# Gate and up weights of each expert loaded whole, one after the other, and multiplied in two 256-column passes

## The chip, the core and the metric

The kernel runs on one core of one Trainium2 chip. The metric is the device time of one execution in microseconds, the median of several runs. TensorE (PE) does the matmuls, VectorE (DVE) and ScalarE (ACT) the elementwise work, GpSimd (POOL) a few copies, and SyncE (SP) issues nearly all transfers from HBM. PE's weight loads have a row of their own in the profile (PEld).

## What is computed

One decoder block: a mixer (two kinds of attention), then a mixture of experts over 256 tokens with 64 experts, of which each token takes 8, and a shared expert; then a final norm. The change touches the experts:

```python
def swiglu(x, w_gate, w_up, w_down):
    return (jax.nn.silu(x @ w_gate) * (x @ w_up)) @ w_down

def moe_ffn(xt, ...):
    ...  # scores, top-k experts eidx and weights wts of each token, rows sorted by expert
    def body(acc, bidx):
        rows = ...; wr = ...; e = blk_expert[bidx]
        ye = swiglu(xt[rows], w_gate_e[e], w_up_e[e], w_down_e[e]) * wr[:, None]
        return acc.at[rows].add(ye.astype(acc.dtype)), None
    routed, _ = lax.scan(body, jnp.zeros_like(xt), jnp.arange(n_blk))
    return routed + swiglu(xt, w_gate_sh, w_up_sh, w_down_sh)
```

Of one expert, gate and up are 1024 x 256 float32 each (1 MB each) and down is 256 x 1024 (1 MB). All 64 experts are read: 201 MB of the 267 MB that the kernel moves.

## The kernel before

The first 270 us or so compute the mixer. Then come the experts in 26 tiles, numbered 0 to 25 here. A tile has 128 rows of PSUM, shared out among two experts (64 + 64 rows, or 96 + 32) or four experts (32 rows each; tiles 3, 7, 11, 15, 20 and 25). Experts are ranked by their load, so that from tile 3 on the expert's number is read from `order` at run time. Ten tiles are worked in four column groups of 32 (the six with four experts, and the four with 96 + 32, whose 96 is cut in three); the other sixteen in two groups of 64.

Two things run side by side.

- **SP** loads weights in program order (`load_tile`, L1086) into a ring of 1 MB buffers (`w8`, L127; 20 of them from tile 3 on, each a [128, 2048] float32 tile: `w`, `whi`, `wlo`, `hh`, `g2r`, `xs`, `gr`, `vv` and `sr` in the profile's names). Expert row p*8+j goes to partition p, so that a partition's gate weights are 8 KB in a row in HBM. `load_gu` (L160) is called for the halves h = 0 and 1: it takes one buffer, and fills its first half with rows j = 4h to 4h+3 of gate and its second half with the same rows of up, each a transfer of 512 KB with 4 KB in a row per partition. So gate and up of an expert are four transfers into two buffers. `load_dn` (L166) loads down as one transfer of 1 MB with 8 KB in a row. A transfer waits until its buffer was last read, and until the transfer eight before it on SP has landed, since SP's transfers take eight completion semaphores in turn.
- **PE** runs the tiles. A tile's steps are, in PE's order: `tile_up` (L1122, eight j, and for each the column groups side by side, a float32 matmul of 512 columns that does gate and up at once), `slot_map` (L1132), `scatter` of the tile before (L1188), `gather` of the next tile's tokens (L1058), the two transposes of `hidden_T` (L1002) and `down` (L1169). `swiglu` (L990) runs on ACT and DVE when the last matmul of `tile_up` is done. A float32 matmul shows in the trace as two matmul records and two weight loads.

The first four j of `tile_up` read the buffers of h = 0, the last four those of h = 1. The last tile loads in smaller pieces (L1095 to L1106), and its down weights in three column cuts (`load_dn_cuts`, `last_down`), so that the end of the kernel waits for little. `late_expert` (L945) is a loop for experts whose tokens overflow their rows; its trip count is zero for these inputs.

Of the kernel before, what the change touches and what calls it, by code (L numbers as in the profile page):

```python
# [25 lines left out]
FF = 256  # L26
# [82 lines left out]
def block_kernel(ctx: ExitStack, tc: tile.TileContext, x, c, norm1_g, norm2_g, w_ada, b_ada, w_in,  # L109
                 w_branch_sb, w_branch_mb, w_out, w_router, router_bias, w_gate_e, w_up_e, w_down_e,  # L110
                 w_gate_sh, w_up_sh, w_down_sh, rel_bias, final_g, const_a, const_m, const_b, out):
    nc = tc.nc
    P = 128
    mm = nc.tensor.matmul
# [9 lines left out]
    def k8(tag, shape, dtype=F32):  # L124
        return wk.tile(shape, dtype, name=tag, tag=tag, bufs=SIZES.get(tag, 1))

    def w8():  # L127
        ring.append(ring.pop(0))
        return k8(ring[-1], [P, 2048])
# [4 lines left out]
    def small(parts=P, width=512, dtype=F32):  # L134
        return wk.tile([parts, width], dtype, name="mg", tag="mg", bufs=4)
# [21 lines left out]

    ss2 = consts.tile([P, 10], F32, name="ss2")

    def load_gu(wg, wu, h):  # L160
        w = w8().rearrange("p (g j f) -> p g j f", g=2, j=4)
        nc.sync.dma_start(w[:, 0], wg.rearrange("(p j) f -> p j f", j=8)[:, 4 * h:4 * h + 4])
        nc.sync.dma_start(w[:, 1], wu.rearrange("(p j) f -> p j f", j=8)[:, 4 * h:4 * h + 4])
        return [w[:, :, j, :] for j in range(4)]

    def load_dn(wd):  # L166
        w = w8().rearrange("p (j n) -> p j n", j=2)
        nc.sync.dma_start(w, wd.rearrange("(p j) n -> p j n", j=2))
        return w

    h2, h2v, hp3, r1, h2T, scores_ = [], [], [], [], [], []
# [23 lines left out]
    with ExitStack() as pa:  # L195
# [534 lines left out]
        for i, ticks in enumerate(ROW_AT):  # L730
            n = 4 + i
# [75 lines left out]
    def rot():  # L807
        return ps.tile([P, 512], F32, name="rot", tag="rot", bufs=3)

    def gub():  # L810
        return ps.tile([P, 512], F32, name="gu", tag="gu", bufs=1)

    def sm(name, shape, dtype=F32, bufs=1):
        return wk.tile(shape, dtype, name=name, tag=name, bufs=bufs)
# [129 lines left out]
    def late_expert(k):  # L944

        no = sm("no", [1, 2], I32)
        nc.sync.dma_start(no[:, 0:1], ranks_d[:, bass.ds(k, 1)])
        rank_ = nc.values_load(no[0:1, 0:1], engines=[EN.SP], min_val=0, max_val=NE - 1)
        nc.sync.dma_start(no[:, 1:2], order_d[:, bass.ds(rank_, 1)])
        col = sm("col", [P, 4])  # L950
        nc.sync.dma_start(col, late_d[:, bass.ds(rank_, 1)].rearrange("p o q -> p (o q)"))
        ev = nc.values_load(no[0:1, 1:2], engines=[EN.SP], min_val=0, max_val=NE - 1)
        wg, wu, wd = (w[0, bass.ds(ev, 1)].rearrange("o a b -> (o a) b") for w in (w_gate_e, w_up_e, w_down_e))
        gu = load_gu(wg, wu, 0) + load_gu(wg, wu, 1)
        wd = load_dn(wd)
        for first in (0, 128):
            one = small().rearrange("p (t s) -> p t s", t=4)[:, 0:2]
            for t in range(NT):
                nc.vector.tensor_scalar(one[:, t], iota1, float(first), col[:, t:t + 1], op0=OP.add, op1=OP.is_equal)
            S = wk.tile([P, NT, 128], BF, name="S", tag="zs", bufs=4)  # L960
            nc.vector.tensor_copy(S, one)
            xg = gather(len(TILES), S)
            pq = rot()
            for t in range(NT):
                nc.tensor.transpose(pq[:, t * 128:(t + 1) * 128], one[:, t], ident)
            for t in range(NT):
                mm(pq[:, 256:257], one[:, t], col[:, 2 + t:3 + t], start=t == 0, stop=t == 1, skip_group_check=True)
            ST = wk.tile([P, 256], F32R, name="ST", tag="e", bufs=3)
            wsl = sm("wsl", [P, 1], bufs=2)
            nc.vector.tensor_copy(ST, pq[:, 0:256])  # L970
            nc.vector.tensor_copy(wsl, pq[:, 256:257])
            p = gub()
            for j in range(8):
                mm(p, xg[:, j], gu[j], start=j == 0, stop=j == 7)
            at = hidden_T(swiglu(p))
            scatter(ST, down(at, [wd], [(0, 128, 0)], wsl))

    shp, shw = {}, {}

    def load_shared():  # L980
        shw["gu"] = load_gu(w_gate_sh[0], w_up_sh[0], 0) + load_gu(w_gate_sh[0], w_up_sh[0], 1)

    def load_shared_down():
        shw["d"] = load_dn(w_down_sh[0])
# [11 lines left out]
    def shared_up(t, j0, j1):  # L996
        if j0 == 0:
            shp[t] = rot() if t else gub()
        for j in range(j0, j1):
            mm(shp[t], h2T[0][:, j, t * 128:(t + 1) * 128], shw["gu"][j], start=j == 0, stop=j == 7)  # L1000

    def hidden_T(sg, at=None):  # L1002
        pt = rot()
# [82 lines left out]
    def load_tile(i):  # L1086
        n = len(TILES[i])
        es = []
        for _, r in TILES[i]:
            if r < NFIX:  # L1090
                es.append([w[0, r] for w in (w_gate_e, w_up_e, w_down_e)])
            else:
                ev = nc.values_load(order[0:1, r:r + 1], engines=[EN.SP], min_val=0, max_val=NE - 1)
                es.append([w[0, bass.ds(ev, 1)].rearrange("o a b -> (o a) b") for w in (w_gate_e, w_up_e, w_down_e)])
        if i == len(TILES) - 1:  # L1095

            gu = [load_gu(e[0], e[1], 0) for e in es]
            ws = [w8().rearrange("p (g j f) -> p g j f", g=2, j=4) for e in es]
            for j in (0, 2):
                for w, e in zip(ws, es):  # L1100
                    for g in range(2):
                        nc.sync.dma_start(w[:, g, j:j + 2],
                                          e[g].rearrange("(p j) f -> p j f", j=8)[:, 4 + j:6 + j])
            for g, w in zip(gu, ws):
                g += [w[:, :, j, :] for j in range(4)]
            return gu, load_dn_cuts([e[2] for e in es])  # L1106
        gu = [[] for s in range(n)]
        for h in range(2):
            for s in range(n):
                gu[s] += load_gu(es[s][0], es[s][1], h)  # L1110
        return gu, [load_dn(e[2]) for e in es]

    def groups(i):

        out, c0 = [], 0
        for s, (cap, _) in enumerate(TILES[i]):
            for n in (32, 32, 32) if cap == 96 else (cap,):
                out.append((c0, n, s))
                c0 += n
        return out  # L1120

    def tile_up(i, xg, gu, between=()):  # L1122
        p = gub()
        for j in range(8):
            if j == 4:
                for f in between:
                    f()
            for c0, n, s in groups(i):
                mm(p[c0:c0 + n, :], xg[:, j, c0:c0 + n], gu[s][j], start=j == 0, stop=j == 7, skip_group_check=True)  # L1129
        return swiglu(p)  # L1130

    def slot_map(i):  # L1132
# [55 lines left out]
    def scatter(ST, ys):  # L1188
        for c, y in zip(HALVES, ys):
            scatter_cut(ST, y, c)  # L1190
# [12 lines left out]


    load_shared()
    shared_up(0, 0, 5)
    tokens_T(1, rot)
    shared_up(0, 5, 6)
# [15 lines left out]
    xg = gather(0, S)  # L1224
# [45 lines left out]
    for i in range(len(TILES)):  # L1270
# [4 lines left out]
        gu, wd = load_tile(i)  # L1275
# [6 lines left out]
        else:  # L1282
# [5 lines left out]
            if i:  # L1288
                xg = gather(i + 1, S)
# [5 lines left out]
        else:  # L1295
            prev = ST, down(at, wd, groups(i), wsl)
            if i == 0:
                xg = gather(i + 1, S)
# [33 lines left out]
```

## Time and profile before

| what | value |
|---|---|
| time, median of 3 runs | 750.12 us (749.75 to 750.17) |
| the profiled execution | 748.62 us, of which its span is 746.5 us |
| PE busy | 696.3 us of the span (93%), 4727 matmul records |
| DMA moved | 266.73 MB, 357 GB/s over the span |
| experts' stage, about 275 us to the end | DMA engines busy throughout, about 410 GB/s |

All times below are microseconds from the span's start. A "busy" PE row means that a matmul is in its pipeline. A DMA share above 1.00 comes of packets that overlap a little on one engine. The landing of a transfer isn't a row of its own, but in the stretch where SP waits for landings the distance of its issues is the distance of the landings.

### The profile page before, as it was taken

The page shows a single profiled execution, that of the slowest core. Times are in us where ns is not written, and L with a number is a line of the kernel's source. Part 1 is how long each engine was busy: PE and PEld are TensorE (multiplying, and loading weights), DVE is VectorE, ACT ScalarE, POOL GpSimd, SP SyncE. Part 2 cuts the span into 40 slices and gives each one's busy share as a digit, 9 for nine tenths or more (in the row PEclk, how much of TensorE's full clock was granted, in tenths as well). Part 3 has the DMA queues.
Part 4 walks back from the last instruction along what each step waited for, and adds up shares of the span by engine and source line. Part 5 has one row for each costly group of instructions (what it writes and reads, how often), then busy time and mean ns, then how long its engine had stood idle before and what let it go on. Part 6 is the DMA issues. An engine that isn't in the chain of part 4 may idle for free.

```text
span 746.5 us, 12489 instructions
## 1 busy us (share of the span) xinstructions
PE 696.3 (93%) x4727; PEld 389.5 (52%) x4727; DVE 312.3 (42%) x663; ACT 202.3 (27%) x332; POOL 25.1 (3%) x37
## 2 busy tenths in 40 slices
PE   3799999999999979999999999999999998899994
PEld 0486677667787645544444444444444453445532
DVE  1365766766667342333333233332242332223323
ACT  2354665465743231111111111011111110111122
POOL 1010001000001050000000000000000000000000
PEclk9999999999999998999999999999999999999998
DMA  9999988776658659999999999999999999999994
GB/s 352 412 380 389 375 285 301 253 270 217 240 210 297 250 216 383 375 382 413 409 414 413 413 410 396 411 411 412 415 412 412 413 412 414 406 410 412 406 333 157
DMA packets 76862, 266.73 MB, mean 357 GB/s; under 512 B 7013, under 2 KB 9221, under 8 KB 67968
## 3 DMA queue, kind: packets, MB, share of 16 engines
q1 hardware_dynamic: 75344, 262.24, 90.9%
q0 software_dynamic: 1312, 3.65, 1.5%
q8 instruction: 39, 0.64, 0.3%
q14 instruction: 23, 0.19, 0.1%
q10 hardware_dynamic: 144, 0.00, 0.0%
HBM read 264.68 MB, written 1.19 MB: 356 GB/s over the span
## 4 chain that ended last, share of the span: by engine, by line
PE 53%; DMA 41%; DVE 2%; ACT 1%; SPq 1%; issue 1%; POOL 1%; DVEq 0%; ACTq 0%
PE gu L1129 9%; PE big L264 7%; PE big L267 7%; PE big L265 7%; DMA w<-in_w_up_e_dram 6%; DMA w<-in_w_gate_e_dram 5%; DMA whi<-in_w_gate_e_dram 5%; PE rot L1069 5%; PE rot L1153 4%; DMA w<-in_w_ada_dram 3%; DMA whi<-in_w_down_e_dram 3%; PE acc L1185 3%; DMA g2r<-in_w_gate_e_dram 3%; DMA vv<-in_w_down_e_dram 2%; PE att L412 2%; DMA g2r<-in_w_up_e_dram 2%
## 5 line engine op out<-in xcount | busy, mean ns | idle before, releaser
L1129 PE MATMUL gu<-w,hl 128*32 128x512 f32 (+1 forms) x552 | 108.1, 594 | 1.5 <-DMA w<-in_w_up_e_dram 1.4
L264 PE MATMUL big<-whi,hh 128*128 128x512 f32 x184 | 75.0, 408 | 1.7 <-ACT whi L384 1.7
L1153 PE MATMUL rot<-w,at 128*32 128x512 f32 (+1 forms) x272 | 69.6, 629 | 5.7 <-DVE at L1008 5.7
L265 PE MATMUL big<-whi,hl 128*128 128x512 f32 x184 | 72.6, 395 | 0.0
L993 DVE TENSOR_TENSOR sg<-sg,gu 128x256 f32<-128x256 f32 x27 | 11.4, 421 | 140.5 <-ACT sg L992 140.5
L1165 ACT ACTIVATE mg<-y 128x512 fp32r<-128x512 f32 x51 | 32.1, 630 | 130.4 <-DVE y L1159 130.4
L1069 PE MATMUL rot<-S,qksb 128*128 128x128 bf16 x600 | 66.4, 219 | 0.0
L1159 DVE SCALAR_TENSOR_TENSOR y<-rot,wsl,gate 128x512 f32<-128x512 f32 (+1 forms) x53 | 39.1, 738 | 65.0 <-PE rot L1153 63.8
L1069 PE MATMUL rot<-S,qkmb 128*128 128x128 bf16 x600 | 66.1, 219 | 0.0
L1129 PEld LDWEIGHTS gu<-w,hl 128*32 128x32 f32 (+1 forms) x552 | 32.3, 121 | 57.5 <-issue 53.2
L246 DVE TENSOR_TENSOR wlo<-w,whi 128x2048 fp32r<-128x2048 f32 x23 | 52.7, 2291 | 20.1 <-ACT whi L245 19.1
L267 PE MATMUL big<-wlo,hh 128*128 128x512 f32 x184 | 54.0, 394 | 0.2 <-DVE wlo L246 0.2
L1185 PE MATMUL acc<-mg,ST 128*128 128x512 f32 x204 | 54.1, 406 | 0.0
L1166 DVE TENSOR_TENSOR mg<-y,mg 128x512 fp32r<-128x512 f32 x51 | 35.3, 693 | 38.5 <-ACT mg L1165 38.5
L1073 ACT ACTIVATE hl<-rot 128x512 f32<-128x512 f32 x26 | 15.5, 597 | 127.9 <-PE rot L1069 127.9
L992 ACT ACTIVATE sg<-gu 128x256 f32<-128x256 f32 x27 | 10.3, 383 | 136.1 <-PE gu L1129 136.1
L1185 PEld LDWEIGHTS acc<-mg,ST 128*128 128x128 f32 x204 | 36.3, 188 | 17.4 <-ACT sg L992 9.1
L245 ACT ACTIVATE whi<-w 128x2048 fp32r<-128x2048 f32 x23 | 43.9, 1910 | 5.0 <-PE big L265 5.0
L1069 PEld LDWEIGHTS <-qksb 128*128 128x128 bf16 x600 | 40.9, 98 | 7.2 <-issue 6.1
L264 PEld LDWEIGHTS big<-whi,hh 128*128 128x128 f32 x184 | 34.9, 190 | 17.1 <-issue 3.8
L1069 PEld LDWEIGHTS <-qkmb 128*128 128x128 bf16 x600 | 42.0, 98 | 0.0
L1129 PE MATMUL gu<-gr,hl 128*64 128x512 f32 (+1 forms) x104 | 39.6, 593 | 0.5 <-DMA gr<-in_w_up_e_dram 0.5
(354 smaller groups left out, 1103.8 us busy)
## 6 DMA issues: line engine op xcount, KB each, us to landing
w<-in_w_gate_e_dram SPq DMA_DIRECT2D x58, 512.0 KB, 12.0
w<-in_w_up_e_dram SPq DMA_DIRECT2D x58, 512.0 KB, 12.3
w<-in_w_down_e_dram SPq DMA_DIRECT2D x28, 1024.0 KB, 12.0
w<-in_w_ada_dram SPq DMA_DIRECT2D x24, 1024.0 KB, 12.5
w<-in_w_in_dram SPq DMA_DIRECT2D x16, 1024.0 KB, 13.0
whi<-in_w_gate_e_dram SPq DMA_DIRECT2D x12, 512.0 KB, 11.9
whi<-in_w_up_e_dram SPq DMA_DIRECT2D x12, 512.0 KB, 12.1
wlo<-in_w_down_e_dram SPq DMA_DIRECT2D x6, 1024.0 KB, 11.3
```

Source lines behind the costliest of these rows:

```text
L245: nc.scalar.activation(hi, w, AF.Copy)
L246: nc.vector.tensor_tensor(lo, w, hi.bitcast(F32), op=OP.subtract)
L264: mm(p, aa[i][0], ww[i][0], start=start and i == 0, stop=False)
L265: mm(p, aa[i][1], ww[i][0], start=False, stop=False)
L267: mm(p, aa[i][0], ww[i][1], start=False, stop=stop and i == n - 1)
L1069: mm(p[:, b * 128:(b + 1) * 128], parts[k][:, half * 4 + b, :], S[:, k * NT // n], start=k == 0, stop=k == n - 1)
L1129: mm(p[c0:c0 + n, :], xg[:, j, c0:c0 + n], gu[s][j], start=j == 0, stop=j == 7, skip_group_check=True)
L1153: mm(py[c0:c0 + w, 0:n], at[:, jj, c0:c0 + w], wd[s][:, jj, o:o + n], start=jj == 0, stop=jj == 1, skip_group_check=True)
L1159: nc.vector.scalar_tensor_tensor(y, py[:, 0:n], wsl, gate2[:, o:o + n], op0=OP.mult, op1=OP.mult)
L1165: nc.scalar.activation(yh, y, AF.Copy)
L1166: nc.vector.tensor_tensor(yl, y, yh.bitcast(F32), op=OP.subtract)
L1185: mm(sums(t, c), m if len(y) > 1 else m.bitcast(F32), part, start=False, stop=stop and k == len(y) - 1, skip_group_check=True)
```

## The change

Each expert's gate becomes one transfer of 1 MB with 8 KB in a row, into a buffer of its own, and so does up. A tile loads the gates of all its experts first, then the ups, then the downs. `tile_up` then does the eight j of gate into columns 0 to 255 of the tile's PSUM bank, and after them the eight j of up into columns 256 to 511: sixteen steps of 256 columns instead of eight of 512. The new function `up_cut` holds one such step; `gu` is now a list of pairs (gate, up) of buffers. What `between` runs (the last tile's `scatter` and `final_gain`, and `by_expert` in tile 0) stands between the passes, after the same number of PE columns as before. The shared expert and the late loop use the same functions. In the last tile gate is loaded whole, and up as j 0 to 3, then 4 and 5, then 6 and 7.

```diff
-    def load_gu(wg, wu, h):
-        w = w8().rearrange("p (g j f) -> p g j f", g=2, j=4)
-        nc.sync.dma_start(w[:, 0], wg.rearrange("(p j) f -> p j f", j=8)[:, 4 * h:4 * h + 4])
-        nc.sync.dma_start(w[:, 1], wu.rearrange("(p j) f -> p j f", j=8)[:, 4 * h:4 * h + 4])
-        return [w[:, :, j, :] for j in range(4)]
+    def load_gu(wg, wu):
+
+        ws = [w8().rearrange("p (j f) -> p j f", j=8) for _ in range(2)]
+        for w, d in zip(ws, (wg, wu)):
+            nc.sync.dma_start(w, d.rearrange("(p j) f -> p j f", j=8))
+        return ws
+
+    def up_cut(p, xg, gu, gs, k):
+
+        g, j = divmod(k, 8)
+        for c0, n, s in gs:
+            mm(p[c0:c0 + n, FF * g:FF * g + FF], xg[:, j, c0:c0 + n], gu[s][g][:, j, :], start=j == 0, stop=j == 7,
+               skip_group_check=True)
...
     def shared_up(t, j0, j1):
         if j0 == 0:
             shp[t] = rot() if t else gub()
-        for j in range(j0, j1):
-            mm(shp[t], h2T[0][:, j, t * 128:(t + 1) * 128], shw["gu"][j], start=j == 0, stop=j == 7)
+        for k in range(2 * j0, 2 * j1):
+            up_cut(shp[t], h2T[0][:, :, t * 128:(t + 1) * 128], [shw["gu"]], [(0, 128, 0)], k)
...
         if i == len(TILES) - 1:
 
-            gu = [load_gu(e[0], e[1], 0) for e in es]
-            ws = [w8().rearrange("p (g j f) -> p g j f", g=2, j=4) for e in es]
-            for j in (0, 2):
-                for w, e in zip(ws, es):
-                    for g in range(2):
-                        nc.sync.dma_start(w[:, g, j:j + 2],
-                                          e[g].rearrange("(p j) f -> p j f", j=8)[:, 4 + j:6 + j])
-            for g, w in zip(gu, ws):
-                g += [w[:, :, j, :] for j in range(4)]
+            gu = [[w8().rearrange("p (j f) -> p j f", j=8) for g in range(2)] for e in es]
+            for g, o, m in ((0, 0, 8), (1, 0, 4), (1, 4, 2), (1, 6, 2)):
+                for w, e in zip(gu, es):
+                    nc.sync.dma_start(w[g][:, o:o + m], e[g].rearrange("(p j) f -> p j f", j=8)[:, o:o + m])
             return gu, load_dn_cuts([e[2] for e in es])
-        gu = [[] for s in range(n)]
-        for h in range(2):
-            for s in range(n):
-                gu[s] += load_gu(es[s][0], es[s][1], h)
+        gu = [[w8().rearrange("p (j f) -> p j f", j=8) for g in range(2)] for e in es]
+        for g in range(2):
+            for w, e in zip(gu, es):
+                nc.sync.dma_start(w[g], e[g].rearrange("(p j) f -> p j f", j=8))
         return gu, [load_dn(e[2]) for e in es]
...
         p = gub()
-        for j in range(8):
-            if j == 4:
+        for k in range(16):
+            if k == 8:
                 for f in between:
                     f()
-            for c0, n, s in groups(i):
-                mm(p[c0:c0 + n, :], xg[:, j, c0:c0 + n], gu[s][j], start=j == 0, stop=j == 7, skip_group_check=True)
+            up_cut(p, xg, gu, groups(i), k)
         return swiglu(p)
```

On SP, a tile of two experts took ten transfers. This is tile 0, whose experts have fixed numbers; in later tiles rows that only set a register stand between. Before:

```order
L162 DMA w_2121<-in_w_gate_e_dram 128x1024
L163 DMA w_2121<-in_w_up_e_dram 128x1024
L162 DMA w_2124<-in_w_gate_e_dram 128x1024
L163 DMA w_2124<-in_w_up_e_dram 128x1024
L162 DMA w_2127<-in_w_gate_e_dram 128x1024
L163 DMA w_2127<-in_w_up_e_dram 128x1024
L162 DMA w_2130<-in_w_gate_e_dram 128x1024
L163 DMA w_2130<-in_w_up_e_dram 128x1024
L168 DMA w_2133<-in_w_down_e_dram 128x2048
L168 DMA w_2135<-in_w_down_e_dram 128x2048
```

The same tile on SP in the changed kernel:

```order
L1113 DMA w_2135<-in_w_gate_e_dram 128x2048
L1113 DMA w_2137<-in_w_gate_e_dram 128x2048
L1113 DMA w_2136<-in_w_up_e_dram 128x2048
L1113 DMA w_2138<-in_w_up_e_dram 128x2048
L176 DMA w_2143<-in_w_down_e_dram 128x2048
L176 DMA w_2145<-in_w_down_e_dram 128x2048
```

Six transfers of 1 MB stand where there were eight of 512 KB and two of 1 MB; the bytes and the count of buffers are the same.

On PE, this is the middle of `tile_up` of tile 20 (four experts), where it passes from the first 4 MB of its weights to the second; `hl` holds the gathered tokens. Before:

```order
L1129 MATMUL gu<-w_5649,hl 32x512
L1129 MATMUL gu<-w_5652,hl 32x512
L1129 MATMUL gu<-w_5655,hl 32x512
L1129 MATMUL gu<-whi,hl 32x512 x2
L1129 MATMUL gu<-wlo,hl 32x512 x2
L1129 MATMUL gu<-hh,hl 32x512
```

The same place in the changed kernel:

```order
L171 MATMUL gu<-w_6015,hl 32x256
L171 MATMUL gu<-w_6017,hl 32x256
L171 MATMUL gu<-whi,hl 32x256
L171 MATMUL gu<-wlo,hl 32x256
L171 MATMUL gu<-w_6016,hl 32x256
L171 MATMUL gu<-whi,hl 32x256
L171 MATMUL gu<-wlo,hl 32x256
L171 MATMUL gu<-hh,hl 32x256
```

The first rows of each are the last step that reads the first 4 MB, the later ones the first step that reads the second 4 MB. The seam stands at the same place in PE's work, and each step has half the columns.

## Rows read from the trace of the kernel before

**Rows 1.** Page, span in 40 slices: busy tenths of the DMA engines, GB/s.

```profile
DMA  9999988776658659999999999999999999999994
GB/s 352 412 380 389 375 285 301 253 270 217 240 210 297 250 216 383 375 382 413 409 414 413 413 410 396 411 411 412 415 412 412 413 412 414 406 410 412 406 333 157
```

**Rows 2.** Windows: stretch, length; busy us and records of each engine; PEclk, DMA share, GB/s.

```profile
340.00:360.00 20.00, 19.48 (x202) 8.67 (x198) 7.11 (x17) 2.88 (x5) 0.00 (x0) 1.00 1.02 412
360.00:540.00 180.00, 172.95 (x1432) 81.84 (x1426) 58.20 (x126) 22.42 (x40) 0.00 (x0) 1.00 1.02 410
...
620.00:660.00 40.00, 34.55 (x271) 16.25 (x268) 10.70 (x23) 3.88 (x7) 0.00 (x0) 1.00 1.02 410
...
710.00:720.00 10.00, 9.48 (x74) 3.58 (x71) 4.05 (x8) 1.86 (x3) 0.20 (x1) 1.00 0.91 310
720.00:730.00 10.00, 8.47 (x58) 3.14 (x59) 0.85 (x2) 2.86 (x4) 0.00 (x0) 1.00 1.04 357
```

**Rows 3.** Chain that ended last, in order of time: start, us, what (from tile 19).

```profile
605.71 6.87 PE gu L1129 x32
...
615.27 2.70 PE rot L1069 x48
...
626.04 14.99 DMA vv<-in_w_down_e_dram
...
641.05 10.05 DMA w<-in_w_up_e_dram
...
723.89 8.11 DMA hh<-in_w_down_e_dram
```

**Rows 4.** Windows, columns as Rows 2: `tile_up` of tile 20, of tile 21.

```profile
622.36:634.67 12.31, 9.25 (x66) 2.47 (x64) 1.96 (x3) 0.63 (x1) 0.00 (x0) 1.00 1.02 416
...
644.62:654.85 10.23, 8.35 (x35) 2.79 (x36) 1.95 (x3) 0.63 (x1) 0.00 (x0) 1.00 1.01 410
```

**Rows 5.** Waits of SP, 300 to 740 us: waiter, awaited: us in total, times, longest.

```profile
SPq L162 <- DMA w<-in_w_down_e_dram: 26.4, 13, 2.1
...
SPq L162 <- PE rot L1153: 15.5, 2, 8.4
```

**Rows 6.** Timeline of SP: start, us, transfer issued (two stretches).

```profile
364.14 0.33 SPq L162 DMA_DIRECT2D g2r<-in_w_gate_e_dram  x1
...
375.64 0.33 SPq L168 DMA_DIRECT2D sr<-in_w_down_e_dram  x1
...
538.07 0.33 SPq L163 DMA_DIRECT2D w<-in_w_up_e_dram  x1
...
548.03 0.33 SPq L163 DMA_DIRECT2D w<-in_w_up_e_dram  x1
```

**Rows 7.** Page: transfers issued, KB each, median us from issue to landing.

```profile
w<-in_w_gate_e_dram SPq DMA_DIRECT2D x58, 512.0 KB, 12.0
...
w<-in_w_down_e_dram SPq DMA_DIRECT2D x28, 1024.0 KB, 12.0
```

**Rows 8.** Engines; instruction queue of the span, and of 360 to 700 us (DMA).

```profile
PE 696.3 (93%) x4727; PEld 389.5 (52%) x4727; DVE 312.3 (42%) x663; ACT 202.3 (27%) x332; POOL 25.1 (3%) x37
...
q8 instruction: 39, 0.64, 0.3%
...
q8 instruction: 21, 0.34, 0.4%
```

**Rows 9.** Timeline of PE: float32 matmuls of 256 columns, two and four groups.

```profile
705.06 0.59 PE L1139 MATMUL rot<-qkmb,ca 64*64 64x256 f32 x4
...
732.29 0.38 PE L1153 MATMUL rot<-hh,at 128*32 128x256 f32 x1
...
732.50 0.59 PE L1153 MATMUL rot<-hh,at 128*32 128x256 f32 x2
```

**Rows 10.** Timeline of PE after a wait for a landing: first and twelfth record.

```profile
538.16 0.14 PEld L1129 LDWEIGHTS gu<-vv,hl 128*32 128x32 f32 x2 [1.62 <-issue]
...
538.24 0.11 PEld L1129 LDWEIGHTS gu<-gr,hl 128*32 128x32 f32 x1
```

More of the change, by code (lines that the diff above doesn't have):

```diff
@@ L953, in late_expert @@
         wg, wu, wd = (w[0, bass.ds(ev, 1)].rearrange("o a b -> (o a) b") for w in (w_gate_e, w_up_e, w_down_e))
-        gu = load_gu(wg, wu, 0) + load_gu(wg, wu, 1)
+        gu = load_gu(wg, wu)
         wd = load_dn(wd)
@@ L972, in late_expert @@
             p = gub()
-            for j in range(8):
-                mm(p, xg[:, j], gu[j], start=j == 0, stop=j == 7)
+            for k in range(16):
+                up_cut(p, xg, [gu], [(0, 128, 0)], k)
             at = hidden_T(swiglu(p))
@@ L980, in load_shared @@
     def load_shared():
-        shw["gu"] = load_gu(w_gate_sh[0], w_up_sh[0], 0) + load_gu(w_gate_sh[0], w_up_sh[0], 1)
+        shw["gu"] = load_gu(w_gate_sh[0], w_up_sh[0])
     def load_shared_down():
@@ L1123, in tile_up @@
         p = gub()
-        for j in range(8):
-            if j == 4:
+        for k in range(16):
+            if k == 8:
                 for f in between:
                     f()
-            for c0, n, s in groups(i):
-                mm(p[c0:c0 + n, :], xg[:, j, c0:c0 + n], gu[s][j], start=j == 0, stop=j == 7, skip_group_check=True)
+            up_cut(p, xg, gu, groups(i), k)
         return swiglu(p)
```

## The prediction

> **What bounds the kernel now.** I read the page's slices first. From about 280 us to 710 us the DMA engines are busy in every slice at about 410 GB/s [rows 1], and by the windows at a share of 1.02 [rows 2]. The reader is to see that the experts' weights are one unbroken stream, which can end earlier only if its bytes pass faster. PE is busy 173 of 180 us in the same stretch [rows 2], so it is nearly bound too, and the question is which of the two ends last. The chain of waits answers it: it runs on PE through tile 19 (`tile_up` 6.87 us there), and from 626 us on transfers, the last of them landing at 723.89 + 8.11 = 732.0 us [rows 3]. The windows of single tiles show what PE loses: `tile_up` took 12.31 us in tile 20 and 10.23 us in tile 21 [rows 4] against 6.87 us where nothing is awaited [rows 3], so 5.4 + 3.4 = 8.8 us of waiting for weights. I estimate 1.5 us more in the last tile. So about 10.3 us is what a much faster stream could give; beyond it PE binds.
>
> What paces the stream? SP waits mostly for landings (26.4 us in its largest group) and for a buffer only early, 15.5 us in two waits [rows 5], while transfers take 12 us from issue to landing [rows 7]: there is always work queued. So the pace of landings is the price of a byte. From 364.14 to 375.64 us SP issues nine transfers after the first, each let go by the landing of a 512 KB piece: 11.50 / 9 = 1.278 us for a piece with 4 KB in a row. From 538.07 to 548.03 us it issues four, each let go by a down of 1 MB with 8 KB in a row: 9.96 / 4 = 2.490 us [rows 6].
>
> **The change part by part.**
>
> *Long rows.* Two pieces of 512 KB take 2 x 1.278 = 2.556 us, one of 1 MB 2.490 us: 0.066 us per MB less, 0.132 us per expert, since gate and up are 2 MB. Gate and up become transfers of the very shape that down has now, into the same buffers, so I take the price of down's rows for them in full. The lower end is nothing (the 2.5% is a property of the down tensor), the upper is the 10.3 us above. Counted up to where PE last waits in the middle of the kernel, tile 21's second half: tiles 3 to 20 hold 46 experts, tile 21 two, so 48 x 0.132 = 6.3 us. (Tiles 0 to 2 are loaded before the stream is unbroken, behind the mixer's own work, and count as nothing.)
>
> [...] The rows show 2.6%, and down's transfers are the same on the same queue, so I go by them.
>
> *Instruction fetch.* This is what the change adds to the stream. Each 256-column step is a matmul of its own, and a float32 matmul is two matmul and two load records: `tile_up` had 16 x 16 + 10 x 32 = 576 matmuls, the shared expert 16, so 592 x 4 = 2368 records more. The run had 4727 + 4727 records of PE and the page counts 39 fetches of instructions [rows 8], so a fetch brings some 240 records, and 2368 are about 10 fetches more, 8 of them before tile 21's weights. What does one cost the stream? In 340 us there were 21, which took 0.4% of 16 engines: 0.004 x 340 x 16 / 21 = 1.04 us of one engine each [rows 8]. If they spread evenly the stream loses 1.04 / 16 = 0.065 us; if they always hit the engine that is last it loses all of it. Between: an expert without disturbance is 2 x 2.556 + 2.490 = 7.60 us for 3.146 MB, 414 GB/s, and the window shows 410 [rows 2], 1% or 3.3 us in 340, so 0.16 us per fetch. I take that: 8 x 0.16 = 1.3 us. Ends: 0.5 and 8.3 us.
>
> *The second pass on PE.* A step of 512 columns takes 6.87 / 16 = 0.429 us per record (sixteen records deep, the groups side by side) [rows 3]. Steps of 256 columns stand in the trace too: with two groups, two steps of 64 x 64 end in 0.59 us, of which the last one's own length is 0.38, so 0.21 us apart; with four groups 732.29 to 732.50 us, also 0.21 [rows 9]. Read as 0.215, two of them are 0.43, the price of the one they replace. I take +0.1 us per tile (ends 0 and 0.3). Until tile 20 PE's waits swallow it; after the last wait five tiles are left, 0.4 us with what falls in the last tile. The weight loads double, but one lasts 0.11 to 0.14 us [rows 10] and lies under a step of 0.21.
>
> *Waits and order.* The first pass needs the gates of all the tile's experts, 1 MB each, where the first four j needed a buffer of 1 MB of each: the same bytes at the same place in the queue, and buffers come free at the same two points. So no new wait, at nothing; the cover is that the seam in `tile_up` stays in its middle. With eight transfers of 1 MB in flight in place of 4.8 MB on average, SP looks further ahead, and waits for buffers more; that costs only if the stream runs dry, and 8 MB in flight say it doesn't. Four fewer issues per tile of two experts save SP 0.33 us each [rows 6], off the path. `swiglu` still waits for the last matmul of the tile, so ACT starts no sooner.
>
> *The last tile.* Now sixteen pieces of 256 KB follow each other there, and with eight in flight the stream thins out: 310 GB/s and 357 GB/s in the last two windows against 410 [rows 2]. Eight of the sixteen become four of 512 KB. The 4 MB of the second half then need about 10.5 us in place of 11.7, an estimate from these rates, so the last weights gain 1 us more than the middle ones. Down's cuts stay. PE comes to them earlier by its own gain alone, so of this I count 0.3 us.
>
> **Sum.** At tile 21's second half the stream is ahead by 6.3 - 1.3 = 5.0 us, which is within the 5.4 + 3.4 us that PE waits there, so PE moves by it. From there PE adds 0.4 us and the last tile gives back 0.3: 5.0 - 0.4 + 0.3, about 4.9 us. The profiled execution, 748.62 us, would become 743.7. The median shown is 750.12, 1.5 us above that execution, so I forecast 750.12 - 4.9 = **745.2 us**.
>
> **The rivals.**
>
> *Fetches eat the gain (slower).* One mechanism: each added fetch holds up one DMA engine, and the landing waits for the last of 16. It decides at 6.3 / 8 = 0.79 us per fetch. For it: 1.04 us is what one takes of its engine. Against it: 21 fetches cost 3.3 us, not 21. At 1.04 us the stream is 8.3 - 6.3 = 2.0 us later, with PE's 0.4 about 752.5 us; at half of that, 0.5 us, it still gains, 747.9.
>
> *PE becomes the bound by issue (slower).* In a tile of four groups `tile_up` goes from 128 to 256 records in 6.9 us, 27 ns each. The longest stretches of the trace show no more than 400 records in 20 us, 50 ns each [rows 2]. If that were the limit of PE's sequencer, such a tile would go from about 330 records in 16.7 us to 460 in 23, 6.3 us more in each of ten tiles, less the 10.3 us of slack: near 800 us. It decides at about 37 ns per record. Against it: after a wait, twelve records start within 0.1 us (538.16 to 538.24 us) [rows 10], and the gather does 48 matmuls with 48 loads in 2.70 us, 28 ns a record [rows 3].
>
> [...]
>
> *The rows don't pay.* If gate and up keep 2.556 us per MB, 1.3 us of fetches and 0.4 us of PE are left: about 751 us, no change. Nothing in the trace speaks for it but that only down has been seen with 8 KB rows.
>
> *More than forecast.* Fetches at 0.065 us, and the disturbances that 4 KB packets meet fall away with them: up to the 10.3 us, 740 us.
>
> **How the numbers follow.** Forecast (742 to 748) 0.62; more than forecast (740 to 742) 0.08; fetches 0.14, of which 0.04 still end more than 0.2% faster, 0.05 within and 0.05 slower; rows don't pay 0.08, of which 0.06 within 0.2% and 0.02 slower; issue limit 0.04, slower; price per matmul 0.04, within. 0.2%, 1.5 us, is about what a measurement of this kernel can tell from no change. So faster 0.62 + 0.08 + 0.04 = 0.74, within 0.05 + 0.06 + 0.04 = 0.15, slower 0.05 + 0.02 + 0.04 = 0.11. The range runs from 740.0, where PE binds, to 750.0, which takes in most of the cases without change.
>
> **What the profile after would show.** Issues of SP in its waiting stretch 2.49 us apart throughout, and 411 to 416 GB/s in the middle windows: the long rows pay. `tile_up` still 6.9 us where nothing is awaited, in tiles of two and of four groups: PE's term is right; 8 us or more in four-group tiles alone would be the issue limit. `tile_up` of tiles 20 and 21 at about 7.5 and 10 us: PE took over the stream's gain. About 49 fetches on the page, and a rate below 408 GB/s with landings at 2.49: the fetches. The forecast is wrong if gate and up land at 2.55 us per MB, or if the stream runs dry between tiles.

## The result and the profile after

| | before | changed |
|---|---|---|
| median of the runs made side by side, us | 749.93 (748.60 to 750.17) | 740.70 (740.62 to 741.19) |
| ratio, with its 95% interval | | 0.9867 (0.9840 to 0.9894) |
| profiled execution, us (span) | 748.62 (746.5) | 740.65 (738.8) |

The kernel became 9.2 us faster. The forecast was 745.2 us, a gain of 4.9: the sign was right and the time lies in the range, but the gain is almost twice the one that was summed up.

The first fence is from the page after the change: the slices of the DMA engines and GB/s, and the queue of instruction fetches (they answer to [rows 1, 8]).

```profile
DMA  9999988777566769899999999999999999999993
GB/s 351 414 386 385 364 262 300 252 266 266 214 212 237 291 229 425 341 381 422 419 420 420 419 419 421 420 422 418 421 419 422 421 419 422 418 421 419 420 346 125
...
q8 instruction: 48, 0.79, 0.4%
```

The second is windows of the changed kernel, with the columns of [rows 2]: the stream's middle, `tile_up` of tile 20 and of tile 21, and two windows near the end of the stream.

```profile
340.00:700.00 360.00, 345.46 (x3677) 211.03 (x3670) 119.58 (x269) 46.05 (x83) 1.60 (x3) 1.00 1.01 420
619.67:626.78 7.11, 7.11 (x134) 4.12 (x136) 1.96 (x3) 0.63 (x1) 0.00 (x0) 1.00 1.01 418
636.96:647.01 10.05, 7.99 (x67) 4.67 (x68) 1.94 (x3) 0.63 (x1) 0.00 (x0) 1.00 1.01 419
700.00:710.00 10.00, 9.48 (x123) 5.50 (x124) 4.10 (x7) 1.86 (x3) 0.20 (x1) 1.00 0.93 348
710.00:720.00 10.00, 9.04 (x105) 4.73 (x97) 1.06 (x4) 2.15 (x4) 0.00 (x0) 1.00 1.01 357
```

The stream moves 420 GB/s where it moved 410 [rows 2], with its engines as full as before (a share of 1.01, where it was 1.02): the same occupation carries more bytes. `tile_up` of tile 20 waits for nothing any more (12.31 us became 7.11 [rows 4]), and tile 21's wait of 3.0 us is what is left (10.05, against 7.08 in the tiles after it).

SP's timeline shows the pace by itself, as in [rows 6]. From the first of these three rows to the last are nine issues, each let go by a landing of 1 MB, gates, ups and downs alike: 22.36 / 9 = 2.484 us.

```profile
600.25 0.33 SPq L1113 DMA_DIRECT2D wlo<-in_w_up_e_dram  x1
...
612.66 0.33 SPq L176 DMA_DIRECT2D vv<-in_w_down_e_dram  x1
...
622.61 0.33 SPq L1113 DMA_DIRECT2D w<-in_w_up_e_dram  x1
```

The chain that ended last has changed sides. Before, it lay on transfers from tile 20 to the last down cut [rows 3]. Now its last transfer is an up of tile 21, landing at 643.29 us (622.61 + 20.69 before rounding), and from there PE runs to the end without waiting for a weight.

```profile
602.74 19.75 DMA hh<-in_w_up_e_dram
...
622.61 20.69 DMA w<-in_w_up_e_dram
...
643.34 3.67 PE gu L171 x30
...
656.89 6.91 PE gu L171 x64
...
707.83 3.59 PE gu L171 x64
```

### The profile page after: what moved, and what is told of

It reads as the page before. It is cut to its first block, busy times and chain, and to the rows that moved or that the text cites. A ratio compares the mean times of both kernels' runs of the same rounds, so it can differ in the third digit from the quotient of the medians.

```text
span 738.8 us, 14329 instructions
## 1 busy us (share of the span) xinstructions
PE 690.3 (93%) x5911; PEld 449.7 (61%) x5911; DVE 312.1 (42%) x663; ACT 202.1 (27%) x332; POOL 25.4 (3%) x37
## 4 chain that ended last, share of the span: by engine, by line
PE 76%; DMA 17%; DVE 3%; ACT 1%; issue 1%; POOL 1%; SPq 0%; DVEq 0%; ACTq 0%
PE gu L171 19%; PE rot L1155 10%; PE rot L1077 8%; PE big L272 7%; PE big L275 7%; PE big L273 7%; PE acc L1187 6%; DMA w<-in_w_up_e_dram 5%; DMA hh<-in_w_up_e_dram 5%; DMA w<-in_w_ada_dram 4%; DMA w<-in_w_down_e_dram 3%; PE att L420 2%; PE rot L1141 2%; PE acc L1032 1%; PE rot L171 1%; DVE at L1016 1%
## 5 line engine op out<-in xcount | busy, mean ns | idle before, releaser
L171 PE MATMUL gu<-w,hl 128*32 128x256 f32 (+1 forms) x1136 | 118.2, 380 | 1.6 <-DMA w<-in_w_up_e_dram 1.2
L171 PEld LDWEIGHTS gu<-w,hl 128*32 128x32 f32 (+1 forms) x1136 | 69.6, 121 | 40.4 <-issue 6.9
L1155 PE MATMUL rot<-w,at 128*32 128x512 f32 (+1 forms) x272 | 67.2, 610 | 5.7 <-DVE at L1016 5.7
L171 PE MATMUL gu<-whi,hl 128*64 128x256 f32 (+1 forms) x208 | 46.4, 380 | 0.0
L171 PE MATMUL gu<-wlo,hl 128*32 128x256 f32 (+1 forms) x256 | 42.7, 379 | 0.0
```

Of the source, the lines that this page charges most:

```text
L171: mm(p[c0:c0 + n, FF * g:FF * g + FF], xg[:, j, c0:c0 + n], gu[s][g][:, j, :], start=j == 0, stop=j == 7, skip_group_check=True)
L1155: mm(py[c0:c0 + w, 0:n], at[:, jj, c0:c0 + w], wd[s][:, jj, o:o + n], start=jj == 0, stop=jj == 1, skip_group_check=True)
```

## The experiments

Two numbers come back in what follows. The **stretch** is the time from the landing of tile 5's last down to that of tile 24's last down, worked out from each transfer's issue and its time to landing: 46 experts' gate and up and 47 downs (the shared expert's among them), the unbroken part of the stream. Its **lateness** sums up the landings in it that came late: those more than 0.12 us over the median spacing of their kind (a piece of gate or up, or a down), each by what it was over that median. The fetches are those of instructions in the whole span, as the page counts them. Stretch and lateness are of one profiled execution, in us, and the time is the median of the runs.

| kernel | gate and up as | fetches | stretch | lateness | time |
|---|---|---|---|---|---|
| before | 512 KB, 4 KB rows | 39 | 358.16 | 6.6 | 749.93 |
| before_again | the same | 39 | 356.09 | 4.3 | 749.39 (one run) |
| short_rows | the same | 48 | 356.82 | 5.0 | 748.72 |
| big_short | 1 MB, 4 KB rows | 48 | 356.60 | 4.5 | 746.55 |
| long_start | 512 KB, 4 KB rows (from tile 5 on) | 48 | 358.00 | 6.3 | 748.75 |
| even_odd | 512 KB, 8 KB rows | 49 | 350.09 | 4.8 | 741.18 |
| changed | 1 MB, 8 KB rows | 48 | 350.25 | 5.0 | 740.70 |
| after_again | the same | 48 | 350.78 | 5.5 | 741.50 |
| cut128_two | the same | 56 | 351.80 | 7.0 | 743.27 |
| two_j | the same | 36 | 348.54 | 3.3 | 736.92 (one run) |
| short_two_j | 512 KB, 4 KB rows | 36 | 357.05 | 5.0 | 747.64 (one run) |

### The rows, or the order? (short_rows)

The main place of the edit; the shared expert's loads and the last tile's gates are split in the same way:

```diff
         for g in range(2):
             for w, e in zip(gu, es):
-                nc.sync.dma_start(w[g], e[g].rearrange("(p j) f -> p j f", j=8))
+                for o in (0, 4):
+                    nc.sync.dma_start(w[g][:, o:o + 4], e[g].rearrange("(p j) f -> p j f", j=8)[:, o:o + 4])
```

> The changed kernel in everything (order of loads, two passes of 256 columns, buffers), but each 1 MB of gate or up comes as two transfers of 512 KB with 4 KB rows again. Theory (long rows pay): pieces land 1.28 us apart instead of 2.485 per MB, 0.07 us per MB, so the stream is 48 x 0.14 = 6.8 us later at tile 21 than in the changed kernel and the time goes back to 748 to 751 us. Rival (the order of loads and passes paid, not the rows): 740 to 742 us. If in addition the nine more fetches of instructions cost what the prediction took (0.16 us each), it is slower than before, 750 to 752.

748.72 us (747.46 to 749.96), 0.9997 of the kernel before (0.9983 to 1.0011). With short rows the whole change is worth nothing that can be measured: the order of the loads, the two passes of PE and the nine more fetches together neither win nor lose. The window of its stream is back at 412 GB/s:

```profile
340.00:700.00 360.00, 343.42 (x3624) 208.03 (x3618) 117.95 (x263) 45.45 (x82) 1.59 (x3) 0.99 1.02 412
```

### Long rows in small transfers, short rows in big ones

small_long and even_odd load each 1 MB as two transfers of 64 partitions, with 8 KB rows; big_short keeps one transfer and takes each partition's 8 KB from two places.

```diff
 # small_long: neighbouring partitions
-                nc.sync.dma_start(w[g], e[g].rearrange("(p j) f -> p j f", j=8))
+                for o in (0, 64):
+                    nc.sync.dma_start(w[g][o:o + 64], e[g].rearrange("(p j) f -> p j f", j=8)[o:o + 64])
 # even_odd: every second partition
+                for o in range(2):
+                    nc.sync.dma_start(w[g].rearrange("(p o) j f -> p o j f", o=2)[:, o],
+                                      e[g].rearrange("(p o j) f -> p o j f", o=2, j=8)[:, o])
 # big_short
+                nc.sync.dma_start(w[g].rearrange("p (h j) f -> p h j f", h=2),
+                                  e[g].rearrange("(h p j) f -> p h j f", h=2, j=4))
```

> The changed kernel, but each 1 MB of gate or up of all tiles except the last comes as two transfers of 512 KB with 8 KB rows (64 partitions each). By the rows: pieces 1.24 us apart, 740 to 742 us. By the number of transfers and the bytes in flight: 748 to 751 us.

1059.64 us (1038.91 to 1074.37): neither theory. The DMA engines are as full as ever and move 236 GB/s. The window from 340 to 990 us:

```profile
340.00:990.00 650.00, 435.97 (x3512) 243.55 (x3507) 112.42 (x251) 43.17 (x77) 1.10 (x2) 0.82 0.96 236
```

An 8 KB packet thus held its engine for 0.96 x 16 x 8192 / 236 = 533 ns on average, down's packets among them; in the changed kernel, by the same sum, 1.01 x 16 x 8192 / 420 = 315. The experiment did not answer its question, so the partitions were dealt out differently.

> As small_long, 512 KB transfers of 8 KB rows, but each takes every second partition in place of 64 neighbouring ones. small_long's 8 KB packets took 533 ns on average where those of whole transfers take 314. If neighbouring partitions were the cause: packets of 314 ns again, pieces 1.24 us apart, 741 to 744 us, between the changed kernel and the 2 to 3 us that the size of the transfer was worth. If it is the half number of rows in a transfer, whichever they are: about 1060 us again.

741.18 us (740.98 to 741.89), 0.9895 (0.9877 to 0.9912). Pieces land 1.24 us apart, and the window:

```profile
340.00:700.00 360.00, 343.59 (x3661) 211.41 (x3654) 118.40 (x267) 45.80 (x82) 1.59 (x3) 1.00 1.01 420
```

So the rows pay, and not the size of the transfers: from short_rows to even_odd the rows double, with as many transfers of as many bytes, each to half of the partitions (the last tile and the shared expert load as in the changed kernel), and the time falls by 7.5 us. From even_odd to the changed kernel, with half as many transfers, it falls by another 0.5, no more than the changed kernel's own two medians differ by (740.70 and 741.50). The packets show the same: from 340 to 700 us a packet of 4 KB lasted 163.8 ns on average in the kernel before, one of 8 KB 314.5 ns in the changed kernel, so that two short ones took 4% more than a long one. The landings show 2.8% (2.555 against 2.485 us per MB); why less is not shown.

> The changed kernel, but gate and up come as one transfer of 1 MB of 4 KB rows (a partition's 8 KB are taken from two places of the matrix; the rows of gate and up are thereby permuted against the tokens, so the experts' products are of other numbers, in the same shapes). Rival tested: not the row length paid but the number of transfers, or the 8 MB in flight in place of 4 to 5. By the rows: as short_rows, 748 to 751 us, a landing every 2.55 us. By the transfers: 740 to 742 us, a landing every 2.485 us.

746.55 us (745.33 to 747.22), 0.9954 (0.9941 to 0.9967), between the two forecasts. Gate and up land 2.555 us apart and the window is at the short rows' rate, as the theory of the rows has it:

```profile
340.00:700.00 360.00, 344.12 (x3630) 208.58 (x3620) 117.66 (x263) 45.43 (x81) 1.59 (x3) 0.99 1.02 412
```

But it is 2.2 us faster than short_rows, with the same pace and the same stretch: it is ahead before the stretch begins (tile 5's last down at 343.00 us against 345.56; two executions of the kernel before differ there by as much, 343.43 and 345.85). long_start was to show whether that is the start.

> Gate and up of tiles 0 to 4 as the changed kernel loads them (1 MB, 8 KB rows), from tile 5 on as short_rows (two pieces of 512 KB, 4 KB rows). It tells where the 2 to 3 us lie that 1 MB transfers gave with rows still short. Theory (they lie where the stream starts anew, in tiles 3 and 4): about 2.5 us less than short_rows, 745.5 to 746.5 us. Rival (they lie all along the stream): only the long rows of tiles 3 and 4 count, 6 experts x 0.14 = 0.8 us less, 747.5 to 748.2 us.

748.75 us (746.05 to 749.67), 0.9985 (0.9972 to 0.9997): the time of short_rows, so the theory that big transfers at the start are worth 2.5 us falls. Its tile 5 landed at 344.29 us, 1.3 ahead of short_rows, and 40 us later (tile 7's first down, 383.87 against 383.83) nothing of that was left. What big_short gains over short_rows is not settled. With long rows the size of the transfers is worth 0.5 us or nothing.

### What does a fetch of instructions cost?

```diff
 # cut128_two (cut128_four: len(gs) == 4)
+        w = 128 if len(gs) == 2 else FF
+        for c in range(0, FF, w):
+            ... the matmuls of a step, w columns from c on
 # two_j, short_two_j, in tile_up
-            up_cut(p, xg, gu, groups(i), k)
+            if i < 3 or k % 8 in (0, 7):
+                up_cut(p, xg, gu, groups(i), k)
```

The kernels that cut to 128 columns compute other numbers than the layer's; their instructions and bytes are all there. two_j and short_two_j leave out twelve of the sixteen steps.

> The changed kernel, but in the sixteen tiles of two column groups each step of tile_up is cut once more, into 128 columns: 16 x 32 more float32 matmuls, 2048 more records of PE each for matmuls and loads together, so 8 or 9 more fetches of instructions (about 57 in place of 48). By the prediction's price of a fetch (0.16 us of the stream) tile 21's weights come 1.1 us later and the time is 741.5 to 742.3 us. By the rival that a fetch costs a whole 1.04 us: 748 to 750 us. If fetches cost the stream next to nothing: 740.5 to 741.2 us. All three take for granted that a step of 128 columns costs half of one of 256; tile_up above 7.2 us in tiles of two groups would show that it does not.

743.27 us (742.20 to 743.81), 0.9909 (0.9886 to 0.9931), 2.6 us more than the changed kernel, between the forecasts of 741.5 to 742.3 and of 748 to 750. The page counts 56 fetches. `tile_up` took 7.16 us from its first start to its last end in tiles of two groups (7.08 in the changed kernel), but the end follows the stream: tile 24's last down lands at 695.73 us against 693.21, 2.5 later, and PE then ends waiting for the last down cut. Of these 2.5 us 1.0 were there before the stretch began. The stretch is 351.80 us against 350.38, the mean of the six executions with 8 KB rows and 48 or 49 fetches (three in the table, last_whole with 349.99, later_four and later_four2 with 350.42 and 350.73), 1.42 us more.

> The changed kernel with four of the sixteen steps of tile_up from tile 3 on (j 0 and 7 of gate and of up; the others are left out). All bytes move, PE has 5 us to spare in each tile, and some 3170 records of PE fall away, 13 fetches fewer (about 35). It measures the stream with fewer fetches. From tile 5's last down to tile 24's last down the changed kernel's stream took 350.3 us, 139 pieces of 2.485 us and 4.9 us of disturbance. At 0.16 us a fetch 348 us; at 0.05 us 349.7 us; at 1.04 us or if all the disturbance is fetches' about 347 us or less. The time falls as far as the end of the stream lets it, to 732 to 738 us.

736.92 us, and the stretch took 348.54 us, 1.84 less than that mean. But not all fetches fall into the stretch. The instruction queue over the stretch of the changed kernel, of cut128_two and of two_j:

```profile
q8 instruction: 29, 0.48, 0.6%
...
q8 instruction: 34, 0.56, 0.6%
...
q8 instruction: 18, 0.29, 0.3%
```

So the price is 1.42 / 5 = 0.28 us per fetch from the one side and 1.84 / 11 = 0.17 from the other, each from a single profile beside six that differ by 0.8 us.

The lateness tells the same more directly. All eleven late landings of the changed kernel come 2.4 to 4.2 us after a fetch began, all nine of its second profile 2.1 to 4.2 and all ten of cut128_two 2.2 to 4.2, though a fetch begins only every 12 us or so in the changed kernel. Per fetch in the stretch the lateness is 5.0 / 29 = 0.17 us there, 7.0 / 34 = 0.21 in cut128_two and 3.3 / 18 = 0.19 in two_j (where one of seven late landings, 0.3 us, follows no fetch). The prediction took 0.16.

> two_j (four of sixteen steps of tile_up from tile 3 on, the others left out, about 36 fetches of instructions) with short_rows' loads. With 48 fetches the stream of short rows took 356.8 and 358.0 us in its two executions between tile 5's and tile 24's last down. If a fetch costs the stream of short rows the 0.14 to 0.19 us that it cost that of long rows, 12 fewer give 355.3 to 356 us. If with short rows it costs nothing over what is there anyway: 356.8 to 358 us. One execution alone tells only a difference of over 2 us for certain.

747.64 us, stretch 357.05. Six executions with short rows have 358.16 and 356.09 (39 fetches), 356.82, 358.00 and 356.60 (48) and this one (36): no order by fetches. They differ by 2 us on their own account, more than six fetches should cost (22 begin in the stretch of the kernel before, 28 in that of short_rows: 1.0 us at 0.17). The late landings tell why. In short_rows all six (5.0 us) come 2.2 to 3.1 us after the start of a fetch. In the kernel before, six of nine follow one (5.0 us) and three do not (1.6 us), and in short_two_j only two of nine do (1.3 of 5.0 us). So short rows are delayed by fetches too, and in some executions by something else besides, which no run here identifies.

### Is PE near a limit of issue?

> The changed kernel, but in the ten tiles of four column groups each step is cut into 128 columns: 256 matmul records and as many loads in the 6.9 us in which the changed kernel issues 128 and 128. This measures the prediction's rival of an issue limit, which the change itself stayed below. If PE issues no faster than the 27 to 28 ns a record seen so far, tile_up takes about 14 us in these tiles, 7 us more in each, and the time is about 740.7 + 10 x 7 - 3 = 805 us. [...] If issue is no limit, 741 us.

754.87 us, neither of the two. The windows of `tile_up` alone in tiles 3 and 4, PE and loads:

```profile
322.90:330.20 7.30, 7.19 (x256) 6.92 (x256) 1.00 0.88 304
339.70:349.00 9.30, 7.38 (x256) 6.84 (x252) 1.00 1.01 418
```

In tile 3 PE issues 512 records in 7.19 us, 14 ns each (28 ns for a matmul record with its load): the rival of an issue limit was wrong by more than a factor of two. But in tile 4 it loses 2 us at one place, and the waits of PE have a row for `tile_up` that no other kernel has. Waits from 300 to 755 us, and the timeline around the pause:

```profile
PE gu L173 <- issue: 10.7, 7, 1.8
```

```profile
344.05 0.29 PE L173 MATMUL gu<-wlo,hl 128*32 128x128 f32 x3
344.07 0.27 PE L173 MATMUL gu<-g2r,hl 128*32 128x128 f32 x1
346.07 0.31 PE L173 MATMUL gu<-wlo,hl 128*32 128x128 f32 x3 [1.72 <-issue]
```

PE stands still from 344.07 to 346.07 us with all its data there. A fetch of its instructions had begun at 343.6, and each of the seven pauses of that row begins 0.3 to 1.0 us after the start of a fetch. The times point to the fetch of its instructions; what held PE up is not shown. The changed kernel has no such pause. This kernel's stretch (359.98 us) says nothing of the price of a fetch: one landing in it came 8.2 us late, and SP often waited for buffers that PE still read.

### What is left, and a better order of tiles

> The changed kernel with the last tile's up weights whole too (1 MB each instead of 512 + 256 + 256 KB). By the trace of the changed kernel PE runs from tile 22 to the end without a wait for a landing: no change, 740.0 to 741.5 us. Rival (the last tile's pieces still set the end): 1 to 2 us slower, since the last up weights can be used only when 1 MB has landed.

741.03 us (740.89 to 741.11), no change. PE no longer waits in the last tile, and how its weights are cut there has stopped to matter.

> The changed kernel without the loads of one tile of two experts (tile 18 multiplies with tile 17's weights, so its products are other numbers): 6 MB less, the stream is 15 us ahead from there on. Theory: in the changed kernel the only wait of PE for a weight behind the middle is 3.0 us in tile 21; without it the time is 740.7 - 3.0 = 737.7 us, and that is what PE alone takes. Rival: PE waits for something else there too, or the last tile's weights still set the end: 739 to 741 us.

736.79 us (736.40 to 738.54), 0.9830 (0.9806 to 0.9855): 3.9 us less than the changed kernel. `tile_up` waits for no weight any more, so this is near PE alone. In its profile tile 16 begins 0.9 us earlier, before the edit can tell, and tile 21 no longer loses its 3.0.

```diff
 # later_four: number of two-expert tiles ahead of each tile of four
-    _n = len(_two) // (len(_q) - _i) if _i else 0
+    _n = (0, 3, 3, 3, 6, 2)[_i]
```

> The changed kernel with its fifth tile of four experts as tile 22 in place of tile 20 (the same tiles in another order). Tile 20's 12 MB are what makes the stream late at tile 21; two tiles later PE has its work ahead while they come. Landings counted on from the changed kernel's trace: no wait left at tiles 20 to 24 (the smallest margin 0.7 us), but the last tile's down cuts would come up to 2.2 us after PE could use them, where they were just in time. So of the 3.0 us 0.8 to 1.5 are gained: 739.2 to 739.9 us. Rival: the stream is what ends last anyway, and the wait is only moved to the end: 740.5 to 741 us.

740.08 us (739.44 to 740.21), a little above the forecast. `tile_up` waits for no weight in tiles 20 to 24, and PE begins the last tile's `tile_up` 4.3 us earlier (703.46 against 707.75 us; 1.0 of it was there at tile 15, up to which the order is the same). There the down cuts now come too late. Run again beside the changed kernel:

> The order of tiles with the fifth tile of four experts as tile 22, once more, now beside the changed kernel on the same chip. If its 0.6 us were real: 740.0 to 740.2 us here with the changed kernel at 740.6 to 740.8. If they were the difference of two chips: the same time.

739.79 us (739.57 to 740.32) against 741.50 (740.67 to 741.93) of the changed kernel on the same chip, with no run of one among those of the other: 1.7 us there, 0.6 by the medians of the other chips. It is the fastest complete kernel of this study. Its chain at the end:

```profile
705.61 3.59 PE gu L171 x64
709.20 2.03 PE acc L1187 x8
711.23 7.39 DMA hh<-in_w_down_e_dram
...
718.64 5.94 DMA hh<-in_w_down_e_dram
...
724.62 1.05 PE rot L1155 x10
```

The wait was moved to the last down cuts, as the rival had it, and with it most of what was won: in later_four 2.9 us, from the start of the last tile to the end of the span (33.91 us against 31.02). What of the gain in time is the order's, and not an earlier start, is about half a microsecond by the two pairs of profiles.

### Two executions of the same kernel

> The kernel before once more, to see how far its stream differs from one execution to the next: its runs spread over 4 us (747.0 to 751.0), those of the changed kernel over 0.6. If the disturbance of the stream (landings over 0.12 us late between tile 5's and tile 24's last down, 6.6 us in the first profile) is what spreads, a slower execution shows more of it and an equally regular pace of 1.28 us otherwise.

749.39 us. Its regular pace is the same 1.28 us, but its stretch took 2.1 us less than in the first profile, with 4.3 us of lateness for 6.6, though its time was 0.8 us longer: it had begun 2.4 us later (345.85 against 343.43 us), and the last up of tile 21 landed at 650.93 against 651.09.

> The changed kernel once more, beside later_four2 on the same chip and with a second profile. Between tile 5's and tile 24's last down the stream took 350.2 us in its first profile and 350.0 to 350.4 in the three kernels that load alike, where the kernel before took 358.2 and 356.1 in two executions. If long rows make the stream repeatable, 350.0 to 350.5 us again and times within 0.6 us of 740.7. If that was luck, a spread of 2 us as before.

Stretch 350.78 us, half a microsecond from the first profile's and a little over the forecast; three of its four runs lie more than 0.6 us from 740.7. The stream of long rows repeats within 0.8 us in six executions, that of short rows within 2.1. All runs of the kernel before spread from 747.0 to 751.0 us, those of the changed one, which are fewer, from 740.6 to 741.9. Long rows alone don't make times repeat: no_load_18's four runs spread over 2.1 us.

## Why the prediction was wrong

The forecast missed by 745.2 - 740.7 = 4.5 us. By its own steps:

- **From the profiled execution to the median, 1.45 us.** The sum gave 743.7 us for the profiled execution; the text then added the 1.5 us by which the median of before lay above its profile. The changed kernel's profile lies on its median (740.65 and 740.70). The median of before lies above its profile because its runs spread over 4 us; the changed kernel's spread less. That step had no row to stand on.
- **Long rows, 0.5 us.** 0.132 us per expert came from 2.556 - 2.490 us per MB. Gate and up land in 2.485 (the timeline above: 2.484), so it is 0.142, over 48 experts 6.8 us in place of 6.3. The runs agree: the stretch fell from a mean of 357.12 us (six executions with short rows) to 350.38, 6.7 us in 46 experts, 0.147 each. The mechanism and the row it was priced from (down's) were right.
- **Instruction fetch, 1.3 us.** The number (49 forecast, 48 counted) and the price (0.16 us; 0.17 to 0.21 by the late landings) were near the mark, the price partly by luck: it shares out 3.3 us of loss read from rates, where the late landings from 360 to 700 us add up to 5.1, of which 3.5 follow a fetch. What failed is that the debit stands alone, as if fetches were all that delays the stream of before. Its profile had 6.6 us of lateness with 22 fetches in the stretch, 1.6 of them in three landings that follow no fetch; the changed kernel has 5.0 with 29, all after fetches. What the added fetches cost was made up by disturbances that fell away. How much of that was this one execution's is not settled: before_again has 4.3 us, of which 0.7 follow no fetch.
- **Waits and order, about 1.0 us.** Costed at nothing, "the same bytes at the same place in the queue". The last up of tile 21 landed at 651.09 us before and at 643.29 after, 7.8 us earlier in place of 5.0. With the two items above 1.0 us remain. The gain at this landing repeats (650.6 to 651.5 us in four executions with short rows in 512 KB, 643.2 to 643.6 in three with long rows in 1 MB; even_odd 644.70), but not its parts: the changed kernel's second profile against before_again has 2.9 us of it already when the stretch begins, the first pair 0.5 (343.43 against 342.96). So the 1.0 us stays open.
- **From tile 21 to the end, right.** Forecast + 0.4 - 0.3 us; the way from that landing to the end of the span was 746.5 - 651.09 = 95.41 us before and 738.8 - 643.29 = 95.51 after. Both terms were smaller than forecast and cancel as these did: `tile_up` without a wait went from 6.87 to 6.91 us where 0.1 more was taken, and the last tile, from the start of its `tile_up` to the end of the span, took 31.03 us before and 31.02 after, so it gave nothing back. The missing 0.3 us lies outside the span (2.12 us before, 1.85 after).

So 1.45 + 0.5 + 1.3 + 1.0 + 0.3 = 4.55. The mechanism held: the stream is priced by the pace of its landings, and PE's waits in tiles 20 and 21 take the gain up (forecast 7.5 and 10 us, measured 7.11 and 10.05). What failed is the step from there to the time: a debit for added fetches with no credit for the other late landings of before, read from one execution, and an offset of one profile carried over to another kernel. The rival "more than forecast" gave the time, but only half of its reason came true: disturbances fell away (1.6 us in this pair of profiles), while a fetch cost about 0.17 us and not 0.065.

Of the other rivals, "the rows don't pay" is refuted by even_odd against short_rows, "fetches eat the gain" by a price of at most 0.28 us where 0.79 would decide, and the limit of issue by cut128_four. For the price per matmul that stands in the chances no run shows a figure; what tile 3 of cut128_four shows is 28 ns for a matmul record with its load (256 of each in 7.19 us). The floor of PE, 740 us in the text, is lower: no_load_18 runs in 736.8. The text counted 1.5 us of waiting in the last tile that doesn't show (the 31.03 us against 31.02 above), and overlooked `tile_up` of tiles 11 and 15, which took 7.83 and 8.83 us before and 7.11 after, waits that a faster stream takes away as well.

## What to carry to other kernels

When a stream of weights has work queued all the time, price a byte by the spacing of its landings for each row length that the trace holds, and lengthen the rows if the longer ones land faster (here 2.485 us per MB with 8 KB rows, 2.555 with 4 KB); number and size of the transfers mattered little here (0.5 us from even_odd to the changed kernel). Before you charge a disturbance to a cause, see in the trace which late landings follow it, and look at a second execution; don't carry the distance of one profile from its median over to another kernel. When the stream catches up, look where PE waits next: here the same tiles in another order gave 0.6 to 1.7 us more by the medians, and about half a microsecond by the profiles.

## What the runs showed of the hardware

- In small_long, where each transfer of gate and up goes to 64 neighbouring partitions, an 8 KB packet held its engine for 533 ns on average (340 to 990 us, down's packets among them). In even_odd, where each goes to every second partition, it was 315 ns by the same sum (340 to 700 us), as in the whole transfers of the changed kernel. Why the neighbours were slow is not shown.
- In tile 3 of cut128_four PE issued a float32 matmul record and its load every 28 ns (256 of each in 7.19 us), but in that kernel it paused seven times in `tile_up`, for up to 1.8 us, "issue" in the waits, each time 0.3 to 1.0 us after a fetch of its instructions had begun.
- The lateness in a stream of 8 KB rows was 0.17 to 0.21 us per fetch of 16 KB of instructions (the changed kernel, cut128_two and two_j), much less than the 1.07 us that the packet of such a fetch lasted (mean of 29 in the changed kernel, 340 to 700 us). It came in single landings, 2 to 4 us after a fetch began: 11 of 29 fetches in the changed kernel were followed by a late one.
- From 340 to 700 us a 4 KB packet lasted 163.8 ns in the kernel before and an 8 KB packet 314.5 ns in the changed one, both to 128 partitions: two short ones took 4% more than a long one of the same bytes.
